# Softmax reciprocals on GpSimd as a power of −1, and neighbourhood scores negated and minimised

## The chip, the core and the metric

The kernel runs on one core of one Trainium2 chip. The metric is device time in microseconds (us) of one execution, and the figure compared is the median of repeated runs. Before the change the median of three runs is 1474.62 us, the lowest 1473.72, the highest 1475.12.

The engines have short names in what follows: PE is TensorE (matrix products), PEld its weight loads, DVE VectorE, ACT ScalarE, POOL GpSimd, and SP is SyncE, which issues most DMAs here. Each engine takes its instructions in one fixed order and waits on semaphores for the results of others.

## What is computed

One inference step of a two-layer transformer trunk for two groups of tokens with the same weights: 128 context tokens (the "prompt") and 512 latent tokens on a grid 64 wide. Layer 0 has two sets of attention heads side by side: 8 heads of MLA (keys and values come from a compressed latent) and 8 heads of two-dimensional neighbourhood attention. Layer 1 has 8 heads of grouped-query attention (GQA). A SwiGLU feed-forward block follows each. Latent tokens also read 128 cached context tokens. All attentions end in a softmax over keys:

```python
def attend_blocked(q, k, v, scale):                       # MLA and GQA, blocks of 128 queries
    s = jnp.einsum('bqkgd,bskd->bkgqs', qi, k).astype(jnp.float32) * scale
    p = jax.nn.softmax(s, axis=-1).astype(v.dtype)
    return jnp.einsum('bkgqs,bskd->bqkgd', p, v)

def neighbourhood_attention(q, k, v, k_ctx, v_ctx, rpb):  # one grid row
    s_band = jnp.einsum('bqhd,bikhd->bhqik', q_r, k_band).astype(jnp.float32) * NA_SCALE
    s_band = s_band + bias.transpose(0, 2, 1, 3)[None].astype(jnp.float32)
    s_band = jnp.where(col_mask[:, None, :], s_band, NEG_INF)
    s_ctx = jnp.einsum('bqhd,bchd->bhqc', q_r, k_ctx).astype(jnp.float32) * NA_SCALE
    p = jax.nn.softmax(jnp.concatenate([s_band, s_ctx], axis=-1), axis=-1).astype(v.dtype)
```

Inputs and outputs are 32-bit floats.

## The kernel before

**Arithmetic and layout.** TensorE multiplies in the type `fp32r`. To keep precision each operand is split into a high part (a copy by ACT) and a low part (the operand less its high part, mostly by DVE), and the helper `mm3` (its products are all recorded at L64) adds three products. `unit` does this for weights: a load issued by SP at L165 into one of three buffers, the copy at L173, the subtraction at L174. The argument `lo="g"` puts the subtraction on POOL; only the key weights of MLA, `wm0` to `wm3`, use it. Activations stand feature-major, 640 tokens (512 latents and 128 context) in two halves of 320.

**The softmax of one head.** A head has four tiles of 128 queries (GQA a fifth of 128 x 128; in the other two, one pair of such prompt tiles for two heads, `prompt_pair`). For each tile:

1. PE makes scores in PSUM (`ns`, `ms`, `gs`).
2. DVE finds the maximum of each row and its negative. In MLA (L990) and for the prompt that is one reduction with a negated result (`mn`); in GQA the negated maximum is also multiplied by a factor (L1864, `gb`). In neighbourhood attention one instruction adds mask and bias to the scores, stores the sums in `np` and keeps their maximum (L784, `nm`), and a second negates it (L787, `nn`).
3. ACT computes the exponential with that negative maximum as a bias and accumulates the sum of the row (`nl`, `ml`, `gl`): L788, L992, L1865. The trace shows the reading of that sum as an instruction of its own, ACTIVATION_READ_ACCUMULATOR.
4. `softmax_tail` (L390 to L393): DVE takes the reciprocal of the sum (L392, `nr`, `mr`, `gr`), and POOL multiplies the tile by it (L393, in place).

One head later PE transposes the weights (L68, helper `tr`) into `nt`, `mt` or `gt`, `pt_split` splits these into a high part on ACT (L401, `nts..h`, `mts..h`) and a low part on DVE (L402, `nts..l`, `mts..l`), and PE multiplies with the values (`no`, `mo`, `go`).

**The order.** For each head, pieces of this work are written down in a fixed string: `NA_ORDER`, `MLA_ORDER` and `GQA_ORDER`. `s0` to `s4` are score tiles with their softmax, `t0` to `t4` transposes with their splits, `v0` to `v4` products with the values, and `q`, `k`, `m`, `w`, `u` are projections and weight units of the next head or stage, put between so that PE has work while the softmax passes through the other engines. A scheduler then places each engine's instructions from that order and its own idea of when each is ready, so an instruction that is removed or moved to another engine also shifts others.

**What else POOL does there.** In neighbourhood attention it adds mask and bias tables (L765, `bm`) and scales or copies queries and keys (L719, L744, L746); at the end of it come the splits of `wm0` and on; in MLA it makes the low parts of the queries (L891, `mql`).

Of the kernel before, what the change touches and what calls it, by code (L numbers as in the profile page):

```python
# [11 lines left out]
F32 = mybir.dt.float32  # L12
F32R = mybir.dt.float32r
AF = mybir.ActivationFunctionType
ALU = mybir.AluOpType
# [3 lines left out]
P = 128  # L19
# [11 lines left out]
GQA_SCALE = 128.0 ** -0.5  # L31
EPS = 1e-6
# [19 lines left out]
def body(ctx, tc, xT, vecs, crow, wm0, wm0g1, wm0g, wm1, wA, wNV, wNA, wMK, wMV, wOA, wGQ, wGK, wGV, wOC,  # L52
# [3 lines left out]
    V, S, G = nc.vector, nc.scalar, nc.gpsimd  # L56
# [13 lines left out]
    main = ctx.enter_context(tc.tile_pool(name="main", bufs=1))  # L70
# [5 lines left out]
    tiny = ctx.enter_context(tc.tile_pool(name="tiny", bufs=6))  # L76
# [12 lines left out]
    def bank(name, kind="m"):  # L89
        if kind == "m":  # L90
            return psp.tile([P, 512], F32, tag="m", bufs=4, name=name)
        return ypool["pool"].tile([P, 512], F32, tag=kind, bufs=ypool["tags"][kind], name=name)
# [41 lines left out]
    make_identity(nc, ident)  # L134
    ones = main.tile([P, P], F32, name="ones")
    V.memset(ones, 1.0)
    eps = main.tile([P, 1], F32, name="eps")
    V.memset(eps, EPS)
    lnsc = main.tile([P, 1], F32, name="lnsc")
    V.memset(lnsc, math.log(GQA_SCALE))  # L140

    sel = main.tile([P, 4], F32, name="sel")
    V.memset(sel, 0.0)
# [245 lines left out]

    def softmax_tail(pt, l, name, n):  # L390
        r = tiny.tile([P, 1], F32, tag="r", name=name + "r")
        V.reciprocal(r, l)  # L392
        G.tensor_scalar(pt[:, :n], pt[:, :n], r, 0.0, ALU.mult, ALU.add)  # L393

    def pt_split(ps, n, pool, name, shape=None):
# [29 lines left out]
    def prompt_pair(vs, o, pool, name, sbank):  # L425
# [6 lines left out]
        def first(r, product):  # L432
            def run(spare=None):
                pss = sbank(f"{name}s{r}")[:, :P] if spare is None else spare[:, 0]
                product(pss)
                m = tiny.tile([P, 1], F32, tag="m2", name=f"{name}m{r}")
                V.tensor_reduce(m, pss, AX.X, ALU.max, negate=True)
                l = tiny.tile([P, 1], F32, tag="l2", name=f"{name}l{r}")
                sl = pt[:, r * P:(r + 1) * P]
                S.activation(sl, pss, AF.Exp, bias=m, accum_out=l)  # L440
                softmax_tail(sl, l, f"{name}r{r}", P)
            return run
# [312 lines left out]
    def na_bias(h):  # L755
        gt = ab.tile([P, 32, 15], F32, tag="gt", bufs=1, name=f"gt{h}")
        row = rpbp[h]
        src = bass.AP(tensor=row.tensor, offset=row.offset + 8, ap=[[15, 16], [1, 8], [1, 480]])
        nc.sync.dma_start(gt.rearrange("p a b -> p (a b)"), src)
        bm = bms[h % 2]  # L760
        for v, n0, k0, o in ((0, 0, 0, 0), (0, 128, 16, 128), (1, 0, 0, 0), (1, 128, 16, 256), (2, 0, 16, 256), (2, 128, 0, 128)):
            n1 = n0 + 128
            g0 = gt[:, 31 - k0, 14:15]
            rev = bass.AP(tensor=g0.tensor, offset=g0.offset, ap=[list(g0.ap)[0], [-15, (n1 - n0) // 8], [-1, 8]])
            G.tensor_tensor(bm[:, v, o:o + P].rearrange("p (a b) -> p a b", b=8), rev,  # L765
                            msk[:, v, n0:n1].rearrange("p (a b) -> p a b", b=8), ALU.add)
        return bm

    def na_scores(h, bm, pts):
        p, r = divmod(h, 2)  # L770
        qh, ql, ks = [t[r] for t in nqk[p]]
        mm = tiny.tile([P, 4], F32, tag="mm", bufs=4, name=f"nm{h}")
        ll = tiny.tile([P, 4], F32, tag="ll", bufs=4, name=f"nl{h}")

        def piece(jj):
            banks = [bank(f"ns{h}_{jj}{i}", "y") for i in range(2)]
            for j in (2 * jj, 2 * jj + 1):
                pss = banks[j % 2]
                k0, cq = P * PLACE[j][0], slice(P * j, P * j + P)
                PE.matmul(pss[:, 0:384], qh[:, cq], ks[:, k0:k0 + 384], start=True, stop=False)  # L780
                PE.matmul(pss[:, 0:384], ql[:, cq], ks[:, k0:k0 + 384], start=False, stop=True)
            for j in (2 * jj, 2 * jj + 1):
                pt = ab.tile([P, 384], F32, tag="np", bufs=8, name=f"np{h}_{j}")
                V.tensor_tensor_reduce(pt, banks[j % 2][:, :384], bm[:, (0, 1, 1, 2)[j], :], 1.0, -3.0e38, ALU.add, ALU.max,  # L784
                                       mm[:, j:j + 1])
                nm = tiny.tile([P, 1], F32, tag="nm", name=f"nn{h}_{j}")
                V.tensor_scalar_mul(nm, mm[:, j:j + 1], -1.0)  # L787
                S.activation(pt, pt, AF.Exp, bias=nm, accum_out=ll[:, j:j + 1])  # L788
                softmax_tail(pt, ll[:, j:j + 1], f"nr{h}_{j}", 384)
                pts.append(pt)  # L790
        return [lambda jj=jj: piece(jj) for jj in range(2)]
# [108 lines left out]
    bm = na_bias(0)  # L900
# [5 lines left out]
    for h in range(8):  # L906
        p, r = divmod(h, 2)
# [6 lines left out]
        if h < 7:  # L914
            bm = na_bias(h + 1)
# [62 lines left out]
    def mla_scores(h, pts, beside):  # L978
        r = h % 2
        ll = tiny.tile([P, 4], F32, tag="ll", bufs=4, name=f"ml{h}")  # L980

        def piece(j):
            qh, ql = mqs[h]
            pss = bank2(f"ms{h}_{j}")
            kh, kl = [t[0] for t in k_tiles(r, h // 2)]
            scores(pss, (qh[:, P * j:P * j + P], ql[:, P * j:P * j + P]), kh, kl)
            if j in beside:
                beside[j](pss[:, :, HT:HT + P])
            nm = tiny.tile([P, 1], F32, tag="nm", name=f"mn{h}_{j}")
            V.tensor_reduce(nm, pss[:, :, :HT], AX.XY, ALU.max, negate=True)  # L990
            pt = cp.tile([P, T], F32, tag="mp", bufs=8, name=f"mp{h}_{j}")
            exps[h, j] = S.activation(halves(pt), pss[:, :, :HT], AF.Exp, bias=nm, accum_out=ll[:, j:j + 1])  # L992
            softmax_tail(pt, ll[:, j:j + 1], f"mr{h}_{j}", T)
            pts.append(pt)
        return [lambda j=j: piece(j) for j in range(4)]
# [36 lines left out]
    for h in range(8):  # L1032
        p, r = divmod(h, 2)
# [886 lines left out]
    _, before = mod_side([(1, wm1[G2:], G2)], None)  # L1920
# [172 lines left out]
```

## Time and profile before

| what | value |
|---|---|
| median of three runs | 1474.62 us (1473.72 to 1475.12) |
| span of the profiled execution, first to last instruction | 1475.7 us |
| instructions in it | 25826 |
| chain that ended last: PE / DVE / DMA / ACT / POOL | 75% / 11% / 5% / 5% / 1% |

The page prints for each engine the time in which it was busy, its share of the span and its number of instructions. A second part cuts the span into 40 equal slices, with the busy tenths of each engine:

```profile
PE   5999999999999999999999999999999999999997
DVE  5877788877998889965997878888899898989976
POOL 0046635420000000000000122220000000000000
PEclk9999999999999999999999999999999999999999
```

Each slice is 36.9 us. POOL works in slices 3 to 9, which hold neighbourhood attention and MLA, and in slices 23 to 27, which hold GQA; elsewhere nearly nothing. PE is busy throughout, and its clock is granted in full. Rows of groups read as line, engine, operation, output and inputs with their shapes, count, then busy time in us and the mean of one in ns, then the idle time of that engine just before these instructions and what ended it. Rows of single instructions begin with the start in us and the duration in us. Numbers in names are heads and tiles; the page and the groups by line leave buffer numbers out.

### The profile page before, as it was taken

What the parts mean: (1) busy time and instruction counts of PE and PEld (TensorE: products, weight loads), DVE (VectorE), ACT (ScalarE), POOL (GpSimd) and SP (SyncE); (2) the same over time, 40 slices, a digit from 0 to 9 for tenths busy, and PEclk for the clock granted to TensorE, in tenths of its full rate; (3) what the DMA queues carried; (4) which work ended last, traced back from release to release, by engine and by line L of the source; (5) the groups of instructions that cost most, each with busy time, mean ns of one, the idle gap of its engine ahead of it and who ended that gap; (6) DMA issues with size and microseconds to landing.
All of it is one profiled execution on the core that took longest, in us unless ns stands there. A gap on an engine that the chain in (4) does not pass through costs nothing.

```text
span 1475.7 us, 25826 instructions
## 1 busy us (share of the span) xinstructions
PE 1440.4 (98%) x9764; PEld 1390.5 (94%) x9764; DVE 1235.6 (84%) x2391; ACT 783.4 (53%) x1539; POOL 176.0 (12%) x270
## 2 busy tenths in 40 slices
PE   5999999999999999999999999999999999999997
PEld 3989978889999999999999999989999999999997
DVE  5877788877998889965997878888899898989976
ACT  5446677853755545531223656672656555555443
POOL 0046635420000000000000122220000000000000
PEclk9999999999999999999999999999999999999999
DMA  9643431025164555568764300115245555548572
GB/s 374 217 153 125 144 115 44 15 90 182 48 214 164 169 167 173 183 232 315 240 224 143 100 30 30 43 39 190 86 167 181 182 175 184 176 145 297 181 267 72
DMA packets 79637, 231.49 MB, mean 157 GB/s; under 512 B 8856, under 2 KB 13240, under 8 KB 79128
## 3 DMA queue, kind: packets, MB, share of 16 engines
q1 hardware_dynamic: 77152, 225.43, 44.8%
q10 hardware_dynamic: 1944, 3.48, 0.7%
q8 instruction: 76, 1.25, 0.3%
q0 software_dynamic: 416, 0.93, 0.2%
q14 instruction: 49, 0.40, 0.1%
HBM read 193.15 MB, written 36.66 MB: 156 GB/s over the span
## 4 chain that ended last, share of the span: by engine, by line
PE 75%; DVE 11%; DMA 5%; ACT 5%; issue 3%; POOL 1%; DVEq 0%; ACTq 0%; SPq 0%; POOLq 0%
PE fg L64 14%; PE fd L64 6%; PE fgo L64 5%; PE fo L64 5%; PE gq L64 4%; PE fu L64 3%; PE fdo L64 2%; PE gs L64 2%; PE go L64 2%; PE nq L64 2%; PE nk L64 1%; PE fuo L64 1%; DVE junk L1660 1%; PE gt L68 1%; DMA wm<-in_wm 1%
## 5 line engine op out<-in xcount | busy, mean ns | idle before, releaser
L1660 DVE SCALAR_TENSOR_TENSOR junk<-wm,cb 128x1024 bf16<-128x1024 f32 x88 | 107.3, 1220 | 6.7 <-DMA wm<-in_wm 5.5
L64 PE MATMUL gq<-h10h,wgq 128*128 128x320 f32 x256 | 66.3, 318 | 0.0
L267 POOL TENSOR_SCALAR h10h<-h10t,gs,mods 128x320 fp32r<-128x320 f32 x4 | 4.0, 992 | 430.8 <-DVE h10t L261 428.5
L1400 ACT ACTIVATE wY<-s 128x1024 fp32r<-128x1024 f32 x38 | 40.3, 1061 | 25.7 <-PE fg L64 21.1
L1928 POOL TENSOR_TENSOR xr<-xw,fn1rs 128x320 f32<-128x320 f32 x2 | 1.7, 858 | 412.9 <-ACT fn1rs L235 412.9
L1400 ACT ACTIVATE wZ<-s 128x1024 fp32r<-128x1024 f32 x38 | 40.1, 1055 | 15.4 <-PE fd L64 10.3
L1401 DVE TENSOR_TENSOR wZ<-s,wZ 128x1024 fp32r<-128x1024 f32 x38 | 46.3, 1220 | 1.4
L1401 DVE TENSOR_TENSOR wY<-s,wY 128x1024 fp32r<-128x1024 f32 x38 | 46.3, 1219 | 0.3
L64 PEld LDWEIGHTS gq<-h10h,wgq 128*128 128x128 f32 x256 | 45.3, 190 | 0.6
L1509 DVE TENSOR_TENSOR sg<-up,sg 128x640 f32<-128x640 f32 x38 | 31.3, 823 | 15.8 <-ACT sg L1508 14.8
L1508 ACT ACTIVATE sg<-fg 128x320 f32<-128x320 f32 x38 | 16.7, 439 | 48.4 <-PE fg L64 48.4
L64 PE MATMUL gq<-h10l,wgq 128*128 128x320 f32 x128 | 39.8, 311 | 0.0
L1530 ACT ACTIVATE p<-fd 128x320 f32<-128x320 f32 x38 | 16.6, 438 | 42.5 <-PE fd L64 42.5
L1865 ACT ACTIVATE gp<-gs,gb,rq 128x640 f32<-128x640 f32 (+1 forms) x40 | 31.8, 796 | 13.4 <-DVE gb L1864 12.0
L64 PE MATMUL fg<-h01E,wW 128*128 128x320 f32 x228 | 36.6, 309 | 1.1 <-DVE g L1540 1.1
L64 PE MATMUL fg<-h01N,wZ 128*128 128x320 f32 x228 | 36.6, 309 | 0.3 <-ACT p L1528 0.3
L64 PE MATMUL fg<-h01C,wY 128*128 128x320 f32 x228 | 36.6, 309 | 0.2 <-ACT u L1534 0.2
L64 PE MATMUL fg<-h11N,wZ 128*128 128x320 f32 x228 | 36.7, 309 | 0.0
L64 PE MATMUL fg<-h01q,wX 128*128 128x320 f32 x228 | 36.7, 309 | 0.0
L64 PE MATMUL fu<-h11q,wX 128*128 128x320 f32 x228 | 36.6, 309 | 0.0
L64 PE MATMUL fd<-h11q,wZ 128*128 128x320 f32 x228 | 36.6, 309 | 0.0
L64 PE MATMUL fd<-h01q,wZ 128*128 128x320 f32 x228 | 36.5, 309 | 0.0
(3421 smaller groups left out, 5313.5 us busy)
## 6 DMA issues: line engine op xcount, KB each, us to landing
wm<-in_wm SPq DMA_DIRECT2D x48, 512.0 KB, 4.3
mraw<-in_wm SPq DMA_DIRECT2D x8, 1024.0 KB, 13.2
mraw<-in_wm SPq DMA_DIRECT2D x14, 512.0 KB, 3.7
wmv<-in_wm0g SPq DMA_DIRECT2D x8, 512.0 KB, 4.0
wm<-in_wm0g SPq DMA_DIRECT2D x8, 512.0 KB, 5.4
ruo<-in_wFO SPq DMA_DIRECT2D x8, 512.0 KB, 4.1
rgo<-in_wFO SPq DMA_DIRECT2D x8, 512.0 KB, 5.5
x<-in_xT SPq DMA_DIRECT2D x8, 320.0 KB, 5.2
```

What stands on the lines that cost most here:

```text
L64: cls.last = nc.tensor.matmul(*a, **k)
L68: cls.last = nc.tensor.transpose(*a, **k)
L267: G.tensor_scalar(h[:, c0:c1], t, self.gsl[:, k, 0:1], self.ml[:, self.sh + k, 0:1], ALU.mult, ALU.add)
L1400: S.activation(h, src, AF.Copy)
L1401: V.tensor_tensor(w_, src, f(h), ALU.subtract)
L1508: last = S.activation(sg[:, 0:HT], g[:, :HT], AF.Silu, scale=-1.0)
L1509: V.tensor_tensor(sg, up, sg, ALU.mult)
L1530: S.activation(p5, b5[:, :HT], AF.Copy)
L1660: V.scalar_tensor_tensor(junk, raw, 1.0, cb[:, c, :], ALU.mult, ALU.mult, accum_out=mods[l][:, j0 + i, c:c + 1])
L1865: gexp[h, j] = S.activation(dst, src, AF.Exp, bias=nb, scale=rq[:, j:j + 1], accum_out=ll[:, j:j + 1])
L1928: G.tensor_tensor(x[k][:, c0:c1], root[1][k], nrm.rs[:, c0:c1], ALU.mult)
```

## The change

Two edits. In `softmax_tail` the reciprocal is no longer taken by DVE: POOL raises the sum to the power −1, with a column of constants −1 as the exponent, in the instruction ahead of its scaling. In neighbourhood attention the instruction at L784 multiplies the scores by −1 before it adds mask and bias (`bm`) and keeps the minimum, where it kept the maximum of scores times 1 plus `bm`; so it stores negated sums, its minimum is the negative of the maximum, and the exponential takes the stored tile with scale −1 and the minimum as its bias. The separate negation goes. Two small constant tiles and the new −1 share one tile. In the diff of the kernel's text:

```diff
-    eps = main.tile([P, 1], F32, name="eps")
-    V.memset(eps, EPS)
-    lnsc = main.tile([P, 1], F32, name="lnsc")
-    V.memset(lnsc, math.log(GQA_SCALE))
+    consts = main.tile([P, 3], F32, name="consts")
+    eps, lnsc, neg = [consts[:, i:i + 1] for i in range(3)]
+    for t, value in ((eps, EPS), (lnsc, math.log(GQA_SCALE)), (neg, -1.0)):
+        V.memset(t, value)
...
     def softmax_tail(pt, l, name, n):
         r = tiny.tile([P, 1], F32, tag="r", name=name + "r")
-        V.reciprocal(r, l)
+        G.tensor_tensor(r, l, neg, ALU.pow)
         G.tensor_scalar(pt[:, :n], pt[:, :n], r, 0.0, ALU.mult, ALU.add)
...
-                V.tensor_tensor_reduce(pt, banks[j % 2][:, :384], bm[:, (0, 1, 1, 2)[j], :], 1.0, -3.0e38, ALU.add, ALU.max,
+                V.tensor_tensor_reduce(pt, banks[j % 2][:, :384], bm[:, (0, 1, 1, 2)[j], :], -1.0, 3.0e38, ALU.add, ALU.min,
                                        mm[:, j:j + 1])
-                nm = tiny.tile([P, 1], F32, tag="nm", name=f"nn{h}_{j}")
-                V.tensor_scalar_mul(nm, mm[:, j:j + 1], -1.0)
-                S.activation(pt, pt, AF.Exp, bias=nm, accum_out=ll[:, j:j + 1])
+                S.activation(pt, pt, AF.Exp, bias=mm[:, j:j + 1], scale=-1.0, accum_out=ll[:, j:j + 1])
                 softmax_tail(pt, ll[:, j:j + 1], f"nr{h}_{j}", 384)
```

The edits shorten the text, so lines past L787 stand two lower afterwards (L788 becomes L786, L990 becomes L988). Three places show how the engines' rows change. The first is POOL at the end of neighbourhood attention, where the scalings of the last head (`np_0` to `np_3`, and `npp3p` for the prompt) stand between the splits of the MLA weights `wm0` and `wm1`. Before:

```order
L393 TENSOR_SCALAR np_0_2384<-np_0_2384,nr_0r 128x384
L174 TENSOR_TENSOR wm_2555<-wm0r,wm_2555 128x768
L393 TENSOR_SCALAR np_1_2392<-np_1_2392,nr_1r 128x384
L393 TENSOR_SCALAR np_2_2431<-np_2_2431,nr_2r 128x384
L393 TENSOR_SCALAR np_3_2439<-np_3_2439,nr_3r 128x384
L393 TENSOR_SCALAR npp3p<-npp3p,npp3r0r 128x128
L174 TENSOR_TENSOR wm_2984<-wm1r,wm_2984 128x768
```

The same place after the change, where the rows at L392 are the powers:

```order
L392 TENSOR_TENSOR nr_0r<-nl_2321,consts 128x1
L393 TENSOR_SCALAR np_0_2336<-np_0_2336,nr_0r 128x384
L392 TENSOR_TENSOR nr_1r<-nl_2321,consts 128x1
L393 TENSOR_SCALAR np_1_2342<-np_1_2342,nr_1r 128x384
L174 TENSOR_TENSOR wm_2499<-wm0r,wm_2499 128x768
L392 TENSOR_TENSOR nr_2r<-nl_2321,consts 128x1
L393 TENSOR_SCALAR np_2_2379<-np_2_2379,nr_2r 128x384
L392 TENSOR_TENSOR nr_3r<-nl_2321,consts 128x1
L393 TENSOR_SCALAR np_3_2385<-np_3_2385,nr_3r 128x384
L392 TENSOR_TENSOR npp3r0r<-npp3l_2421,consts 128x1
L393 TENSOR_SCALAR npp3p<-npp3p,npp3r0r 128x128
L174 TENSOR_TENSOR wm_2920<-wm1r,wm_2920 128x768
```

A power stands ahead of each scaling, and the split of `wm0` stands behind two scalings where it stood behind one.

The second place is ACT at the same point. L401 makes the high parts of transposed weights, L846 copies a cached key, L788 is the exponential, L173 the high part of a weight. Before:

```order
L401 ACTIVATE nts_0h<-nt_0_2400 128x512
L401 ACTIVATE nts_1h<-nt_1_2409 128x512
L401 ACTIVATE npp2pth<-npp2t 128x256
L846 ACTIVATE ckph<-ckvr_753 128x128
L788 ACTIVATE np_0_2384,nl_2369<-np_0_2384,nn_0_2386 128x384
L173 ACTIVATE wm_2555<-wm0r 128x768
L788 ACTIVATE np_1_2392,nl_2369<-np_1_2392,nn_1_2394 128x384
L401 ACTIVATE nts_2h<-nt_2_2463 128x512
```

ACT there after the change:

```order
L401 ACTIVATE nts_0h<-nt_0_2348 128x512
L401 ACTIVATE nts_1h<-nt_1_2357 128x512
L786 ACTIVATE np_0_2336,nl_2321<-np_0_2336,nm_2320 128x384
L786 ACTIVATE np_1_2342,nl_2321<-np_1_2342,nm_2320 128x384
L401 ACTIVATE npp2pth<-npp2t 128x256
L844 ACTIVATE ckph<-ckvr_753 128x128
L173 ACTIVATE wm_2499<-wm0r 128x768
L401 ACTIVATE nts_2h<-nt_2_2407 128x512
```

Both exponentials move ahead of two smaller copies and of the copy of `wm0r`, and read the minimum `nm` itself.

The third place is DVE between the first and the second head of MLA. L990 is the row maximum, L889 a step of the queries, L476 and L867 are low parts. Before:

```order
L990 TENSOR_REDUCE mn_3_2953<-ms_3_2946 128x1
L392 RECIPROCAL mr_2r<-ml_2869 128x1
L990 TENSOR_REDUCE mn_0_2974<-ms_0_2967 128x1
L392 RECIPROCAL mr_3r<-ml_2869 128x1
L889 TENSOR_TENSOR mqt_2993<-mq_2981,tq 128x320
L476 TENSOR_TENSOR oNs0l<-oN_1177,oNs0h 128x640
L392 RECIPROCAL mr_0r<-ml_2964 128x1
L990 TENSOR_REDUCE mn_1_3004<-ms_1_2997 128x1
L392 RECIPROCAL mr_1r<-ml_2964 128x1
L867 TENSOR_TENSOR kTl_2542<-mk_3011,kTh_2540 64x512
```

DVE there after the change:

```order
L988 TENSOR_REDUCE mn_3_2889<-ms_3_2882 128x1
L988 TENSOR_REDUCE mn_0_2910<-ms_0_2903 128x1
L887 TENSOR_TENSOR mqt_2929<-mq_2917,tq 128x320
L476 TENSOR_TENSOR oNs0l<-oN_1177,oNs0h 128x640
L988 TENSOR_REDUCE mn_1_2940<-ms_1_2933 128x1
L865 TENSOR_TENSOR kTl_2486<-mk_2947,kTh_2484 64x512
```

The four reciprocals are gone and the rest keeps its order. PE's order changes at a few places at the end of MLA only, and that of SP's queue not at all.

## Prediction, made before the changed kernel ran

> **What bounds the kernel now.** First the busy shares on the page, then a table of three stretches of time in which the softmaxes run: neighbourhood attention (112 to 212 us), MLA (222 to 320) and grouped-query attention (850 to 990). Columns: window, length, and busy time of each engine with its count.
>
> ```profile
> PE 1440.4 (98%) x9764; PEld 1390.5 (94%) x9764; DVE 1235.6 (84%) x2391; ACT 783.4 (53%) x1539; POOL 176.0 (12%) x270
> ...
> 112.00:212.00 100.00, 96.98 (x725) 86.98 (x724) 77.80 (x261) 69.28 (x187) 60.09 (x113) 0.98 0.39 129
> 222.00:320.00 98.00, 93.58 (x607) 82.95 (x607) 85.17 (x180) 77.63 (x179) 49.51 (x56) 1.00 0.09 28
> 850.00:990.00 140.00, 138.44 (x931) 130.67 (x930) 115.70 (x254) 93.47 (x216) 32.99 (x40) 0.99 0.10 31
> ```
>
> TensorE (PE) is the engine that fills the program. In the three stretches it is idle for 3.0, 4.4 and 1.6 us, 9.0 together. That is roughly what a lighter VectorE (DVE) can win: the change touches nothing outside them but two constants at the start. GpSimd (POOL) looks free over the program, 12%, but is at 60% in the first stretch and 51% in the second.
>
> Next, what PE waits for inside the stretches. First and second stretch, in this order; columns: who waits, for what, total us, times, longest.
>
> ```profile
> PE no L64 <- DVE nts_0l L402: 1.7, 1, 1.7
> PE mk L64 <- DVE nm L784: 0.9, 1, 0.9
> ...
> PE ms L64 <- ACT mp L992: 1.5, 2, 1.0
> PE mo L64 <- DVE mts_4l L402: 1.4, 3, 1.1
> PE mo L64 <- DVE mts_3l L402: 0.6, 3, 0.2
> PE mo L64 <- DVE mts_0l L402: 0.5, 2, 0.3
> ```
>
> So where PE stands still, DVE (splitting transposed weights into high and low parts) or ScalarE's exponential is late. The chain of waits between 222 and 320 us shows this more sharply:
>
> ```profile
> by line: ACT mp L992 11.3%; issue 10.7%; DVE mn L990 9.2%; PE mo L64 7.6%; PE ms L64 7.2%; PE mt L68 6.2%; PE mq L64 3.5%; PE mk L64 3.2%; PE oa0a L64 3.0%; DVE mts_0l L402 3.0%; DVE mts_4l L402 2.8%; ACT oaw L173 2.4%; ACT mts_2h L401 2.3%
> ...
> 240.44 0.16 DVE mpp0r1r L392
> ...
> 301.45 0.16 DVE mr_2r L392
> ```
>
> The MLA stretch is set by a relay: scores on PE, row maximum on DVE (`mn`), exponential on ACT (`mp`), split on DVE (`mts`). Its chain runs through eight reciprocals (first and last shown, 0.14 to 0.17 us each, 1.3 together). The chains of the other two stretches hold three each.
>
> **The change part by part.** Reciprocals leave DVE: 40 in each stretch, 120 in all.
>
> ```profile
> L392 DVE RECIPROCAL nr_0r<-nl x8: 144/152/164, 115.2 to 203.0; 128x1 f32<-128x1 f32 x8
> ...
> L392 DVE RECIPROCAL gr_2r<-gl x8: 155/164/165, 859.3 to 983.6; 128x1 f32<-128x1 f32 x8
> ...
>   ACT gp L1865: 9.7, 12
>   ACT np L788: 4.1, 12
>   ACT mp L992: 3.8, 8
> ```
>
> At about 0.158 us each that is 120 x 0.158 = 19 us of DVE time. The last three rows are idle time of DVE in front of a reciprocal, while ACT finishes the sum it needs: 9.7, 4.1 and 3.8 us in the third, first and second stretch. DVE takes its work in order, so this idle time goes too, unless the next instruction waits for the same ACT result.
>
> *MLA.* On the chain: -1.3 us. Of the 3.8 us of idle time I count 0.3, since DVE makes up about that share of the chain (from the row by line: 15% in its three large DVE entries, the rest in small ones): -1.2, an estimate whose ends are 0 and -3.8.
>
> *GQA.* Three reciprocals on the chain: -0.5 us. The 9.7 us of stalls lie beside a PE that is 98.9% busy; I count them at nothing, and were that cover gone, PE's 1.6 us of idle time would be the price.
>
> *Neighbourhood attention.* Three more on the chain: -0.5 us. Here 32 negations also go (minimum of negated scores in place of maximum, a constant swapped in an instruction that stays, and a scale of -1 in an exponential that was there):
>
> ```profile
> L787 DVE TENSOR_SCALAR nn<-nm x32: 126/148/155, 114.1 to 205.6; 128x1 f32<-128x1 f32 x32
> ```
>
> That is 4.7 us of DVE, and each exponential starts a DVE step earlier. No negation stands on the chain and PE is 97% busy there: nothing, with PE's 3.0 us of idle time as the far end.
>
> *What POOL gets.* 40 powers in each stretch, each followed by the scaling that was there already and now waits for POOL's own result. No row of this trace shows a power, so bounds from the nearest rows:
>
> ```profile
> L2073 POOL MEMSET const-float32-0.0<- 128x1 f32 x1 | 0.1, 98 | 0.2 <-issue 0.2
> ...
> L765 POOL TENSOR_TENSOR bm<-gt,msk 128x128 f32<-128x128 f32 x48 | 22.7, 499 | 13.2 <-DVE nm L784 9.4 <-DMA gt<-in_rpbp 3.5
> L891 POOL TENSOR_TENSOR mql<-mqt,mqh 128x320 fp32r<-128x320 f32 x16 | 14.0, 873 | 10.3 <-ACT mqh L890 10.3
> ...
> L174 POOL TENSOR_TENSOR wm<-wm2r,wm 128x768 fp32r<-128x768 f32 x1 | 1.8, 1834 | 10.4 <-ACT wm L173 10.4
> ```
>
> The lower end is 0.10 us, one column written. From 320 to 768 columns a two-input operation grows by 961 ns, 2.15 ns a column, which leaves 0.19 us for one column of addition. A power is more work than an addition; the nearest row is the 0.50 us one, and I take **0.4 us**, with 1.83 as the far end. Load of POOL: 60.1 + 16 = 76 of 100 us, 49.5 + 16 = 66 of 98, 33 + 16 = 49 of 140. It fits.
>
> Latency decides too, since the transposes need the scaled weights. The last scaling of a head against the first transpose after it, second head boundary of MLA:
>
> ```profile
> 242.18 0.19 ACT L992 ACTIVATION_READ_ACCUMULATOR mp<-ms,mn 128x1 f32 x1
> 243.30 0.15 DVE L392 RECIPROCAL mr_3r<-ml 128x1 f32<-128x1 f32 x1
> 243.55 0.80 POOL L393 TENSOR_SCALAR mp<-mp,mr_3r 128x640 f32<-128x640 f32 x1 [2.48 <-DVE mr_3r L392]
> 244.89 0.27 PE L68 MATMUL mt<-ident,mp 128*128 128x128 f32 x1
> ...
> 304.79 0.19 ACT L992 ACTIVATION_READ_ACCUMULATOR mp<-ms,mn 128x1 f32 x1
> 305.56 0.80 POOL L393 TENSOR_SCALAR mp<-mp,mr_3r 128x640 f32<-128x640 f32 x1 [1.32 <-DVE mr_3r L392]
> 306.03 0.83 PE L68 MATMUL mt<-ident,mp 128*128 128x128 f32 x5
> ```
>
> At the first of these the reciprocal stood behind other DVE work, and 1.18 us passed from sum to scaling; at the second 0.58. In the new order it is a hand-over (about 0.10), the power, and a hand-over (about 0.09): 0.59. So at 0.4 us the path is no longer than now. Only the last head had a shorter one (0.43): +0.2 us. MLA together: -1.3 - 1.2 + 0.2 = **-2.3 us**.
>
> *What moves.* POOL's split of the weights `wm0` stands behind two scalings now instead of one, and ACT's copy for it behind two exponentials. Behind it hangs a load:
>
> ```profile
> 191.64 0.62 ACT L788 ACTIVATE np<-np,nn 128x384 f32<-128x384 f32 x1
> 192.24 0.85 ACT L173 ACTIVATE wm<-wm0r 128x768 fp32r<-128x768 f32 x1
> ...
> 193.32 1.82 POOL L174 TENSOR_TENSOR wm<-wm0r,wm 128x768 fp32r<-128x768 f32 x1
> 195.17 0.33 SPq L165 DMA_DIRECT2D wm1r<-in_wMK  x1
> 198.60 0.85 ACT L173 ACTIVATE wm<-wm1r 128x768 fp32r<-128x768 f32 x1
> 199.47 0.60 ACT L401 ACTIVATE nts_0h<-nt 128x512 fp32r<-128x512 f32 x1
> ...
> 202.37 0.50 PE L64 MATMUL no<-nts_0l,nv 128*128 128x512 f32 x1 [1.67 <-DVE nts_0l L402]
> ```
>
> POOL's split ends, SyncE's queue issues the load of `wm1r` into the freed buffer, ACT copies it, and only then copies `nts_0h`, for whose low half PE waits 1.67 us. In the new order ACT does two exponentials (0.7 each with the read of the sum) and two small copies before `wm0r`, so that copy ends near 194.2 rather than 193.1; POOL's split then ends near 196.1 rather than 195.1. One microsecond late, on a path with nothing to absorb it: **+1.0 us**, with 0 and +2 as ends. The stretch gives -0.5 + 1.0 = +0.5.
>
> **Sum:** -2.3 - 0.5 + 0.5 = **-2.3 us**. The profiled span of 1475.7 us becomes 1473.4; it lies 1.1 above the median of the timed runs, 1474.62, so the forecast there is **1472.3 us**.
>
> *A rule weighed.* Two rows from the MLA stretch:
>
> ```profile
> 276.49 1.21 DVE L174 TENSOR_TENSOR oaw<-oaw1r,oaw 128x1024 fp32r<-128x1024 f32 x1
> 276.67 1.70 POOL L393 TENSOR_SCALAR mp<-mp,mr_2r 128x640 f32<-128x640 f32 x1 [1.58 <-DVE mr_2r L392]
> ```
>
> The scaling takes 1.70 us beside a DVE operation on two SBUF tiles, and 0.80 in the rows above. The Trainium skill, page "SBUF — State Buffer", section "SBUF: two separate sides", says that GpSimd and a VectorE operation with two SBUF inputs share one port pair, which whoever starts first holds for the whole instruction. The trace agrees: the scaling ends 0.67 us after DVE does. By that rule a power can be held as well; one hold of up to 1.2 us at the end of a head would make the sum -1.1 in place of -2.3.
>
> **The rivals.** *POOL becomes the bound (slower).* In the first stretch it has 39.9 us left for 40 powers, so this decides from 1.0 us a power. At 1.2 us: 108.1 of 100, +8.1; the path from sum to transposes is 0.8 us longer, more than the two last head boundaries can take, +1.8; `wm0` waits for two powers, +2.5; the gains of 3.1 stay: +9.3, 1484 us. At the far end, 1.83 us, POOL needs 133 and 123 us in the first two stretches, +55 us. For it: a power is computed by an engine whose plain additions are three times a reciprocal here. Against: one column only.
>
> *The relay tightens (faster).* If DVE's idle time in MLA goes entirely (3.8 in place of 1.2) and the earlier exponentials win half of PE's 3.0 us in the first stretch and of its 1.6 in the third: -2.3 (the forecast) - 2.6 - 2.3 = -7.2, 1467.4; half of the way beyond the forecast, -4.8, is its middle: 1469.8 us. For it: each exponential of the first stretch stands a negation earlier.
>
> *PE hides it.* PE is over 95% busy in all three, and what one wait loses the next gains: -0.3, 1474.3 us.
>
> That the change does not do what it says is ruled out by the order: the powers stand on POOL, the reciprocals are gone from DVE, no negation is left.
>
> **How the numbers follow.** Forecast 0.40 (1470.7 to 1473.6), the relay tightens 0.24, PE hides it 0.13, POOL the bound 0.23. A change under 0.2%, 2.9 us, is about what a measurement of this kernel cannot tell from none. The forecast's own range crosses it: 0.16 faster, 0.24 same. Faster: 0.16 + 0.24 = 0.40; same: 0.24 + 0.13 = 0.37; slower: 0.23. The range runs from 1467.4 to 1484, leaving out some 0.05 below and 0.1 above.
>
> **What would show it.** POOL rows `nr`, `mr`, `gr` at L392 near 0.4 us; DVE busy time near 24 us lower (19 + 4.7); no DVE idle time put down to sums at L392; the MLA stretch some 2 us shorter; the load of `wm1r` about 1 us later against the first `mk`, and PE's wait at `nts_0l` longer. Wrong, if a power takes 1 us or more, if PE waits for POOL's scalings, or if the stretches stay the same length though DVE is lighter.

## The result and the profile after

The changed kernel takes 1481.0 us, median of five runs (1479.05 to 1483.22). Five runs of the kernel before had their median at 1474.62 us (1473.72 to 1477.61). The ratio is 1.0038, with a 95% interval of 1.0027 to 1.0048: **slower by 0.38%, about 5.6 us** (the two medians lie 6.4 us apart), where 1472.3 us, 2.3 us less, had been forecast.

The profiled execution after the change, its span and busy times, and the three stretches (same columns as before the change):

```profile
span 1477.2 us, 25760 instructions
...
PE 1440.6 (98%) x9764; PEld 1390.1 (94%) x9764; DVE 1224.7 (83%) x2240; ACT 785.5 (53%) x1539; POOL 244.8 (17%) x390
```

```profile
112.00:212.00 100.00, 96.26 (x726) 85.99 (x725) 69.07 (x181) 68.80 (x184) 81.64 (x151) 1.00 0.40 130
222.00:320.00 98.00, 91.60 (x587) 81.12 (x586) 81.60 (x141) 77.39 (x178) 70.93 (x96) 1.00 0.09 28
850.00:990.00 140.00, 138.71 (x946) 131.35 (x945) 115.50 (x219) 93.22 (x217) 56.59 (x80) 1.00 0.10 32
```

DVE became lighter, as meant, but by 10.9 us over the program (8.7 in the first stretch) and not by the forecast's 24. The forecast added up the durations of the instructions that go. Short instructions of DVE overlap with their neighbours in the trace; in the kernel before, for instance (start, duration, instruction):

```profile
122.16 0.27 DVE L713 SCALAR_TENSOR_TENSOR nql<-nq,nqh 64x128 fp32r<-64x128 f32 x1
122.36 0.14 DVE L392 RECIPROCAL nr_0r<-nl 128x1 f32<-128x1 f32 x1
122.42 0.13 DVE L787 TENSOR_SCALAR nn<-nm 128x1 f32<-128x1 f32 x1
122.48 0.67 DVE L402 TENSOR_TENSOR nts_1l<-nt,nts_1h 128x512 fp32r<-128x512 f32 x1
```

The 120 reciprocals last 18.9 us in all, but in only 9.7 us of these is no other row of DVE busy. POOL went from 60 to 82 us of the first 100 and from 50 to 71 of the second 98. PE lost 2 us of work in the second stretch, so it stood still there for longer.

The powers, as rows of the group by line (minimum, median and maximum in ns; first and last start in us), one of each attention:

```profile
L392 POOL TENSOR_TENSOR nr_1r<-nl,consts x8: 542/548/558, 118.8 to 206.9; 128x1 f32<-128x1 f32 x8
...
L392 POOL TENSOR_TENSOR mr_1r<-ml,consts x8: 547/549/961, 230.2 to 312.7; 128x1 f32<-128x1 f32 x8
...
L392 POOL TENSOR_TENSOR gr_1r<-gl,consts x8: 542/547/552, 861.0 to 983.3; 128x1 f32<-128x1 f32 x8
```

A power takes 0.55 us. Who waits for POOL's scalings, in the first two stretches and just past them (who, for what, total us, times, longest):

```profile
PEld nt L68 <- POOL np L393: 3.0, 3, 1.6
PE nt L68 <- POOL np L393: 2.3, 2, 1.4
```

```profile
PEld mt L68 <- POOL mp L393: 3.6, 3, 1.9
PE mt L68 <- POOL mp L393: 2.8, 2, 1.7
```

PE and its weight loads wait together, so the two rows of a pair are not to be added. In the kernel before, the only such row is in MLA:

```profile
PEld mt L68 <- POOL mp L393: 0.2, 1, 0.2
```

The wait is new, and it has few places: PE waits 0.87 us at 123.6 us, 1.43 at 203.0, 1.68 at 238.2 and 1.12 at 318.6. The third of them, on POOL's timeline at the start of MLA (start, duration, instruction):

```profile
230.17 0.55 POOL L392 TENSOR_TENSOR mr_1r<-ml,consts 128x1 f32<-128x1 f32 x1
230.82 0.80 POOL L393 TENSOR_SCALAR mp<-mp,mr_1r 128x640 f32<-128x640 f32 x1
231.59 0.56 POOL L392 TENSOR_TENSOR mpp0r0r<-mpp0l,consts 128x1 f32<-128x1 f32 x1
232.24 0.37 POOL L393 TENSOR_SCALAR mpp0p<-mpp0p,mpp0r0r 128x128 f32<-128x128 f32 x1
232.58 1.85 POOL L174 TENSOR_TENSOR wm<-wm3r,wm 128x768 fp32r<-128x768 f32 x1
234.38 0.55 POOL L392 TENSOR_TENSOR mr_2r<-ml,consts 128x1 f32<-128x1 f32 x1
235.03 0.88 POOL L393 TENSOR_SCALAR mp<-mp,mr_2r 128x640 f32<-128x640 f32 x1
235.89 0.86 POOL L889 TENSOR_TENSOR mql<-mqt,mqh 128x320 fp32r<-128x320 f32 x1
236.72 0.55 POOL L392 TENSOR_TENSOR mr_3r<-ml,consts 128x1 f32<-128x1 f32 x1
237.36 0.80 POOL L393 TENSOR_SCALAR mp<-mp,mr_3r 128x640 f32<-128x640 f32 x1
```

```profile
238.22 0.77 PE L68 MATMUL mt<-ident,mp 128*128 128x128 f32 x5 [1.68 <-POOL mp L393]
```

Apart from 0.10 us between a power and its scaling, POOL is never idle in these rows: its work stands in a queue. The sum that `mr_3r` needs was read off by 232.99 us, and its power starts at 236.72. Ahead of it stood the split of `wm3`, another tile's power and scaling, and `mql`. From the end of a power to the start of its scaling there are 0.10 us, so each tile takes POOL 0.55 + 0.10 = 0.65 us more than it did.

**What a single trace hides.** The span grew by only 1.5 us between the two profiled executions, a quarter of the measured loss. The profiled execution after the change was the fastest of its five (1479.05 us, with a span of 1477.2). If the span before, 1475.7, is likewise 1.85 us short of the timed figure, it stands for about 1477.5 us, near the slowest of the five before. Two traces can't give the total, then, and single stretches need care with the granted clock (third column from the end). Below are the kernel before (two rows), the one after, and the run that only negates the scores, where it is 1.00:

```profile
180.00:212.00 32.00, 29.25 (x214) 25.14 (x214) 28.38 (x88) 27.73 (x72) 16.64 (x26) 0.95 0.35 112
850.00:1000.00 150.00, 148.44 (x994) 139.84 (x993) 120.47 (x261) 97.52 (x223) 32.99 (x40) 0.99 0.13 45
```

```profile
20.00:50.00 30.00, 28.55 (x230) 24.13 (x230) 22.48 (x63) 13.72 (x31) 0.00 (x0) 0.89 0.90 338
```

```profile
850.00:1000.00 150.00, 148.63 (x1004) 139.84 (x1003) 120.76 (x262) 97.66 (x223) 32.94 (x40) 1.00 0.15 50
```

In a dip the clock grants PE 1.5 to 3.5 us less than the length of the window (32 x 0.05 = 1.6 in the first row, 150 x 0.01 = 1.5 in the second, 30 x 0.11 = 3.3 in the third). Which of these three windows have one changes from execution to execution; the rows of nines on the page before are too coarse to show its two dips. Before and after, the dips come to about the same, 3.1 and 3.3 us, so they don't explain the small growth of the span; but they fall into different stretches. GQA looked 1.6 us shorter after the change; all of that was the dip of the trace before.

### The profile page after: what moved, and what is told of

The parts are those of the page before. It is cut to its first block, busy times and chain, and to the rows that moved or that the text cites. A ratio compares the mean times of both kernels' runs of the same rounds, so it can differ in the third digit from the quotient of the medians.

```text
span 1477.2 us, 25760 instructions
## 1 busy us (share of the span) xinstructions
PE 1440.6 (98%) x9764; PEld 1390.1 (94%) x9764; DVE 1224.7 (83%) x2240; ACT 785.5 (53%) x1539; POOL 244.8 (17%) x390
## 4 chain that ended last, share of the span: by engine, by line
PE 82%; DVE 6%; ACT 4%; DMA 4%; POOL 2%; issue 2%; DVEq 0%; ACTq 0%; SPq 0%; POOLq 0%
PE fg L64 19%; PE fd L64 9%; PE fgo L64 5%; PE fo L64 5%; PE fu L64 4%; PE gq L64 3%; PE fdo L64 2%; PE gs L64 2%; PE go L64 2%; PE nk L64 2%; PE fuo L64 1%; PE gt L68 1%; DMA mraw<-in_wm 1%; PE nq L64 1%; PE mod L64 1%
## 5 line engine op out<-in xcount | busy, mean ns | idle before, releaser
L64 PE MATMUL fg<-h11q,wX 128*128 128x320 f32 x228 | 36.5, 309 | 0.0
```

Source lines behind the costliest of these rows:

```text
L64: cls.last = nc.tensor.matmul(*a, **k)
```

## The experiments

Two accounts stood against each other at first. Q: GpSimd's queue is what costs. R: what costs is the order, since without the negation the scheduler puts ACT's exponentials of neighbourhood attention ahead of other work. Each edit below is against the changed kernel.

**The negated scores alone** (`neg_only`):

```diff
-        G.tensor_tensor(r, l, neg, ALU.pow)
+        V.reciprocal(r, l)
```

> The neighbourhood scores are negated and minimised as in the change, the reciprocals stay on VectorE. Theory Q (GpSimd's queue is what costs: a power of 0.55 us and a hand-over of 0.1 ahead of each scaling, on an engine that was 60% busy): no power, no loss; 1472.5 to 1475 us, no wait of PE for a scaling (POOL np or mp, L393) over 0.3 us. Rival R (the order: without the negation the scheduler puts ACT's exponentials ahead of its splits and weight copies in neighbourhood attention, and that is what costs): most of the loss of 5.6 to 6.4 us is here, 1479 to 1482 us.

Measured: 1477.05 us beside 1476.28 for the kernel before on the same chip, ratio 1.0004 (0.9995 to 1.0012). No loss that can be told from none, where R had 1479 us and more: R falls. The time is 2 us above Q's range too, but the kernel before ran slower there as well, and PE's waits for scalings are as short as before (0.2 us of PEld, one place).

**The powers alone** (`pow_only`): the tensor_tensor_reduce, the negation and the exponential of the kernel before are put back.

> All reciprocals go to GpSimd as powers, the maximum is still negated by an instruction of its own. Q: slower than before by about what the full change loses, 1479 to 1483 us, with waits of PE for scalings of 3 us or more together. R: the order is nearly that of before, so 1473 to 1476 us.

Measured: 1483.45 us beside 1476.28, ratio 1.0043 (1.0028 to 1.0059). The loss is the powers'. The negation's removal is worth nothing measurable, with the powers or without.

**The powers by stage** (`pow_na`, `pow_mla`, `pow_gqa`), each with the negated scores:

```diff
-        G.tensor_tensor(r, l, neg, ALU.pow)
+        G.tensor_tensor(r, l, neg, ALU.pow) if name[0] == "n" else V.reciprocal(r, l)
```

> The negated scores, and powers on GpSimd in neighbourhood attention alone; MLA and GQA keep VectorE's reciprocals. Q: the loss of neighbourhood attention and the first scalings of MLA behind its backlog, without the gain of some 1.7 us that the trace shows in GQA: 1478 to 1481 us. R: 1479 to 1482 us, like the negated scores alone.

> The negated scores, and powers on GpSimd in MLA alone. Q (GpSimd's queue): the wait of 1.9 us for the first head's scalings, behind the split of a weight, and 1.1 us more at the last head, less what VectorE wins: ratio to before 1.001 to 1.002, and the three stages alone (NA +3.7 us, this, GQA 0) add up to the full change's 5.6. If MLA gains what was forecast (-2.3 us), 1472 to 1475 us.

> The negated scores, and powers on GpSimd in GQA alone, where GpSimd has work for 33 of 140 us. Q: no loss in the first two stretches, and GQA shorter by 1 to 2 us as in the trace of the full change: 1471.5 to 1474 us. R: the loss by order less GQA's gain, 1477 to 1480 us.

Measured: neighbourhood attention 1479.61 us, ratio 1.0025 (1.0013 to 1.0037); MLA 1477.78 us, 1.0010 (1.0000 to 1.0020); GQA 1476.58 us, 1.0000 (0.9991 to 1.0010). The first two are where Q had them. The gain that R and Q both allowed GQA, 1 to 2 us, isn't there. The waits for scalings in the two that lose, neighbourhood attention first:

```profile
PEld nt L68 <- POOL np L393: 3.4, 3, 2.0
```

```profile
PEld mt L68 <- POOL mp L393: 4.1, 4, 2.1
```

**The price of the operation** (`mult`). The multiplication leaves the softmax undivided:

```diff
-        G.tensor_tensor(r, l, neg, ALU.pow)
+        G.tensor_tensor(r, l, neg, ALU.mult)
```

> The full change with a multiplication of the sum by -1 in place of the power, on the same engine at the same place; the weights are then scaled by the negated sum, so no softmax is divided. If the price is that of the power's function, a row takes 0.1 to 0.25 us instead of 0.55, and by Q the loss falls to less than half: 1475.5 to 1478 us. If it is what any instruction of one column costs on GpSimd, rows stay near 0.5 us and the time at 1480 to 1482 us.

Measured: 1474.97 us beside 1475.72, ratio 0.9993 (0.9984 to 1.0002).

```profile
L392 POOL TENSOR_TENSOR mr_1r<-ml,consts x8: 185/191/193, 226.7 to 308.7; 128x1 f32<-128x1 f32 x8
```

With the order of every engine unchanged, an instruction of 0.19 us in place of 0.55 takes the whole loss away, more than Q had expected. The stretches agree, at full clock in both traces: 109.8 us in neighbourhood attention and 99.6 in MLA, against 111.2 and 101.6 in the full change. PEld waits for scalings of neighbourhood attention for 1.0 us instead of 3.0:

```profile
PEld nt L68 <- POOL np L393: 1.0, 1, 1.0
```

It is the power's duration, 0.36 us above a multiplication's, that counts.

**Other work taken off POOL.** Against Q stood P: the way of each tile itself is longer, whether POOL is crowded or not. First the additions of mask and bias (`bias_dve`):

```diff
-            G.tensor_tensor(bm[:, v, o:o + P].rearrange("p (a b) -> p a b", b=8), rev,
+            V.tensor_tensor(bm[:, v, o:o + P].rearrange("p (a b) -> p a b", b=8), rev,
```

> The full change, with the 48 additions of mask and bias (0.5 us each) on VectorE, so GpSimd has some 24 us less to do in neighbourhood attention. Q: the powers no longer stand behind them, the median wait of a power for GpSimd there falls from 1.9 us to under 0.5, PE's waits at 122 and 124 us go, 1477 to 1479.5 us. Rival P (not the queue but the longer way of each tile itself, power and hand-over, 0.65 us, is what costs): 1480 to 1482.5 us.

Measured: 1477.14 us beside 1475.72, ratio 1.0004 (0.9995 to 1.0012). POOL's busy time in the first stretch fell to 70 us. PE's waits near 122 and 124 us are gone; one, at 199 us behind the split of `wm0`, is left (a power of 1.52 us stands ahead of it too), and the median wait of a power for POOL fell from 1.9 us to 0.9, not to 0.5:

```profile
PEld nt L68 <- POOL np L393: 2.0, 1, 2.0
```

Then the splits of MLA's key weights (`wm_dve`):

```diff
-            wmk[p] = unit(wMK[p], 768, f"wm{p}", lo="g")
+            wmk[p] = unit(wMK[p], 768, f"wm{p}", lo="v")
```

> The full change, with the four low parts of MLA's key weights (1.83 us each on GpSimd) on VectorE. Q: PE's waits for scalings of 1.7 us at 203 us and 1.9 us at 238 us, which stood behind these splits, go or shrink below 0.6: 1477.5 to 1479.5 us. P: nothing changes, 1480 to 1482.5 us.

Measured: 1478.69 us beside 1475.72, ratio 1.0020 (1.0010 to 1.0029). The time is as Q had it, but the two waits of PE only shrank, to 1.2 and 1.1 us: behind the split stood more powers and scalings. Both together (`relief`):

> The full change, with both the mask additions and the weight splits on VectorE. Q (GpSimd's queue): one by one they took 5.0 and 2.7 us off the loss of 5.6 us (ratios 1.0004 and 1.0020 against 1.0038); if the waits they remove are different ones, both together reach 0.998 to 1.000 of before, 1472.5 to 1476 us. If they removed the same waits, 1.0003 or more, 1476 to 1478 us.

Measured: 1474.95 us beside 1475.88, ratio 0.9989 (0.9980 to 0.9998). P would have kept the loss, so P alone can't be the account. But not every wait of PE for a scaling is gone; neighbourhood attention first:

```profile
PE nt L68 <- POOL np L393: 0.7, 1, 0.7
PE mt L68 <- POOL mp L393: 2.2, 2, 1.1
```

The control (`neg_bias_dve`) has VectorE's reciprocals and the additions on VectorE:

> The control: negated scores, reciprocals on VectorE, and the mask additions on VectorE too. Q: there are no powers to stand behind them, so it is like the negated scores alone, ratio 0.9995 to 1.001. If moving the additions is a gain of its own, whatever the reciprocals do, 0.996 to 0.998, and the run that moved them says nothing of a queue.

Measured: 1474.56 us beside 1475.88, ratio 0.9989 (0.9980 to 0.9997), between the two ranges. So the additions moved are worth 0.15% where there are no powers (1.0004 to 0.9989) and 0.34% where there are (1.0038 to 1.0004); only the difference, some 2.8 us, can be the powers' standing behind them, and the four intervals together leave nearly 3 us to each side of it. With the additions moved, the powers still cost 0.15% (1.0004 against 0.9989). With the splits moved as well, `relief` is level with the control at 0.9989, though MLA is 0.9 us longer in its trace and neighbourhood attention 0.9 us shorter; what the splits on VectorE are worth without powers was not run.

**The middle heads of MLA** (`pow_mid`), where POOL has no backlog:

```diff
-        G.tensor_tensor(r, l, neg, ALU.pow)
+        G.tensor_tensor(r, l, neg, ALU.pow) if name[:3] in ("mr2", "mr3", "mr4", "mr5", "mr6") else V.reciprocal(r, l)
```

> The negated scores, and powers on GpSimd for MLA's third to seventh heads alone, where in the traces a power waits 0.08 us for GpSimd and a tile's way is 1.53 us from sum to scaled weights instead of 1.24. Q: nothing lost, the stretch within 0.4 us of that with VectorE's reciprocals, ratio 0.9995 to 1.0008. P (the longer way of a tile): five eighths of MLA's loss of 1.5 us or so, ratio 1.0010 or more. Were the forecast's relay right, a gain of some 1.4 us: 0.999.

Measured: 1475.9 us beside 1475.88, ratio 0.9996 (0.9987 to 1.0004). The ratio speaks against P (1.0010 or more) and can't tell Q from the forecast's relay; the stretch can. Its length runs from the first start of a score product to the last start of a value product of the last head. The rows give these for the run that only negates, for this run, and for the full change:

```profile
L64 PE MATMUL ms<-kTh,mqh x48: 302/309/418, 220.7 to 299.6; 128*128 128x320 f32 x48
...
L64 PE MATMUL mo<-mts_4l,mv x8: 392/471/503, 244.4 to 321.1; 128*128 128x512 f32 x8
```

```profile
L64 PE MATMUL ms<-kTh,mqh x48: 302/309/414, 219.9 to 297.6; 128*128 128x320 f32 x48
...
L64 PE MATMUL mo<-mts_4l,mv x8: 392/476/503, 243.5 to 318.9; 128*128 128x512 f32 x8
```

```profile
L64 PE MATMUL ms<-kTh,mqh x48: 302/309/416, 224.5 to 304.0; 128*128 128x320 f32 x48
...
L64 PE MATMUL mo<-mts_4l,mv x8: 392/423/494, 249.2 to 326.1; 128*128 128x512 f32 x8
```

That is 100.4, 99.0 and 101.6 us. Powers in five heads win 1.4 us; powers in all eight lose 1.2. Q had allowed 0.4 us either way. In these traces, the forecast's relay was right for the middle heads; over all runs with VectorE's reciprocals in MLA the stretch lies between 99.9 and 100.4 us.

**The best that the runs point to** (`mid_bias`): the edits of `pow_mid` and `bias_dve` together.

> The best the runs point to: negated scores, mask additions on VectorE, powers on GpSimd for MLA's third to seventh heads alone. The additions moved gave 0.9989 with VectorE's reciprocals; the middle heads' powers gave 1.2 us in the MLA stretch of the trace (0.9996 against 1.0004). Q: the two add, ratio 0.9975 to 0.9987, 1471.5 to 1474 us where the kernel before runs at 1475.5. If the stretch's gain is only in that trace, 0.9988 to 0.9995.

Measured: 1474.58 us beside 1476.42, ratio 0.9987 (0.9975 to 0.9999), with an MLA stretch of 98.7 us. It beats both kernels, the one before by 0.13%, just clear of the noise; from the additions moved alone (0.9989) it can't be told.

The lengths of the three stretches in the traces, worked out from such rows (first `ns` to first `ms`; first `ms` to last `mo`; first to last `gs`). A star marks a granted clock below 1.00 inside the stretch:

| run | neighbourhood | MLA | GQA |
|---|---|---|---|
| before | 110.2* | 99.9 | 133.3* |
| neg_only | 109.1 | 100.4 | 131.5 |
| neg_bias_dve | 108.6 | 100.0 | 131.4 |
| pow_only | 113.9* | 101.5 | 133.1* |
| full change | 111.2 | 101.6 | 131.7 |
| pow_na | 113.8 | 100.1 | 131.5 |
| pow_mla | 109.5* | 102.1 | 131.5 |
| pow_gqa | 111.6* | 100.3 | 131.7 |
| bias_dve | 108.9 | 101.6 | 131.7 |
| wm_dve | 112.2 | 100.8 | 131.7 |
| relief | 107.7 | 100.9 | 131.6 |
| mult | 109.8 | 99.6 | 131.5 |
| pow_mid | 108.6 | 99.0 | 132.9* |
| mid_bias | 108.3 | 98.7 | 131.5 |

## Why the prediction was wrong

**The step that failed** is the sentence "It fits" after the sum of POOL's load, and with it the point "from 1.0 us a power" from which POOL would decide. The wait of PE for POOL's scalings was therefore put at nothing; that such waits would show the forecast wrong, it had said itself. Both rest on an average over a stretch: 60 us busy and 40 powers in 100 us. The 76 us that the text worked out became 82, not far off. But the sums of a head's four tiles come in bursts: in neighbourhood attention all four within 1.8 us for the first head (116.5 to 118.3), and mostly two by two, 0.6 us apart, for the later ones. Each tile now takes POOL 0.55 + 0.10 + 0.59 = 1.24 us instead of 0.59. Two take 2.5 us and four 5 us, more behind additions or a weight split. A power waited a median of 1.9 us for POOL in neighbourhood attention, and the way from sum to scaled weights grew from 1.9 to 3.6 us on average (2.4 with the scores negated and the reciprocals on DVE). So POOL decided at 0.55 us a power, with 82 of 100 us busy. The rival had the right engine; it too reckoned with a load above 100%, and so set the threshold too high. That its 1484 us, worked out for 1.2 us a power, lies near the 1481.0 measured is luck, and so is it that the range, which ran up to it, holds the result.

**The power's price**: 0.4 us was taken between 0.10 and 1.83; it is 0.55, and the hand-over from the power to its scaling, 0.10, was counted as latency only, not as time of POOL. The estimate of 0.19 us for one column of a plain two-input operation was right to the hundredth (the multiplication's 0.191).

**MLA, -2.3 us**: +1.2 to +1.6 us in the table (100.0 to 100.4 without powers, 101.6 with all). The gain of the shorter relay exists, 1.3 to 1.4 us for five heads (`pow_mid` against `neg_only`, `mid_bias` against `neg_bias_dve`); taken over eight heads that would be 2.1 to 2.2 us, an estimate near the forecast's 2.3. What was left out is the two ends. The second head boundary, where the old and the new way were compared, is a place where POOL is free; the first is not (the 1.68 us above), and at the last head PE waits 1.12 us for a scaling, for the reason given under the held instructions below.

**GQA, -0.5 us**: +0.2 us (131.6 to 131.7 with powers there, 131.4 to 131.5 without, traces with full clock). That the 9.7 us of stalls were hidden behind PE was right.

**Neighbourhood attention, +0.5 us**: +2.1 us against `neg_only`, and more in `wm_dve` (+3.1) and `pow_na` (+4.7). The late split of `wm0` came, further than reckoned: it starts at 198.00 us, 4.7 later than before, of which 2.1 had been lost ahead of the stretch, so 2.6 in place of 1.0. But PE's wait at `nts_0l` didn't grow; it fell from 1.67 to 0.4 us, since PE had already waited 1.43 us one step earlier, for the scalings behind that split. The negations were worth nothing, as forecast.

**Held instructions**, which the forecast weighed at up to 1.2 us and left out of its sum, come as the rows before the change showed them. In a middle head:

```profile
256.07 1.21 DVE L174 TENSOR_TENSOR oaw<-oaw0r,oaw 128x1024 fp32r<-128x1024 f32 x1
256.28 1.40 POOL L392 TENSOR_TENSOR mr_2r<-ml,consts 128x1 f32<-128x1 f32 x1 [1.18 <-ACT mp L990]
```

The power ends 0.40 us after DVE's operation on two SBUF tiles. This agrees with the Trainium skill, page "SBUF — State Buffer", section "SBUF: two separate sides", that whoever starts first holds the port. The same hold is in the run with the middle heads' powers (1.41 us at 250.59 us), and they win all the same. Of the 120 powers 16 are held like this by 0.1 us or more, 10 us in all, and as many of the 120 multiplications in `mult`, 9 us in all, without a loss. At the last head of MLA, though, two held scalings stand right ahead of a wait of PE:

```profile
315.22 1.42 POOL L393 TENSOR_SCALAR mp<-mp,mr_2r 128x640 f32<-128x640 f32 x1
316.61 0.54 POOL L392 TENSOR_TENSOR mr_3r<-ml,consts 128x1 f32<-128x1 f32 x1
317.04 0.82 DVE L476 TENSOR_TENSOR oMs0l<-oM,oMs0h 128x640 fp32r<-128x640 f32 x1 [0.27 <-ACT oMs0h L475]
317.26 1.27 POOL L393 TENSOR_SCALAR mp<-mp,mr_3r 128x640 f32<-128x640 f32 x1
318.58 0.33 PE L68 MATMUL mt<-ident,mp 128*128 128x128 f32 x1 [1.12 <-POOL mp L393]
```

Unheld they take 0.80 us each, so holding makes up 1.1 us of the way to PE's wait of 1.12 us; in `mult` no scaling of the last head's four tiles is held, and PE doesn't wait there. Ahead of the wait at 203.0 us, holding adds 0.7 us (a power takes 0.74 us, a scaling 1.14); ahead of those at 123.6 and 238.2 us it adds nothing. No run takes the holding alone away, so its share of the loss is an estimate from these rows.

The other way round, powers could hold DVE. Group by group, the operations of DVE that the full change and `neg_only` share last 0.4 us longer in all in the full change in neighbourhood attention, 0.1 us shorter in MLA, and 2.8 us longer in GQA, where nothing was lost. So this is not what the change costs.

**The point of departure**: the forecast took the profiled execution as 1.1 us above the median. A timed figure is 1.85 us above the span of the same execution in the run after the change, so like for like the execution was some 3 us above, about what its two dips of the clock took. The forecast is a difference, and its error doesn't come from there. Two small slips don't either: 0.3 of 3.8 us is 1.1 and not 1.2, and the gains named in the text come to 3.3 and not the 3.1 used for the rival.

**What stays open.** The stages' ratios add up to 1.0035 with the negated scores' 1.0004 counted three times over, 1.0027 with it counted once, against the full change's 1.0038; the intervals, 0.001 to each side, allow that, and nothing finer was measured. In the traces, the three stretches of the full change are together 3.5 us longer than those of `neg_only`, where the ratios differ by 5 us; the rest is not placed. Why neighbourhood attention is 2.6 us longer with powers there alone (113.8) than in the full change (111.2) stays open; its trace has a wait of PE of 1.41 us for `nts_0h` at 141.8 us that the full change lacks. Why moving the additions helps where there are no powers was not tested. A scaling of neighbourhood attention starts 1.4 us after its reciprocal on average in `neg_only` and 0.4 us after it in `neg_bias_dve`, so there was a queue on POOL before any power came.

## What to carry to other kernels

Before work goes to an engine with a low busy share, look at the moments at which it arrives: add the new instruction and its hand-over to the burst, with the longest instruction that can stand ahead of it, and compare with the slack of whoever waits. A short operation moved to a lightly used engine can cost more there than it did on the crowded one: here 0.65 us of a queue in place of a 0.16 us instruction that half overlapped with its neighbours. Read the granted clock beside any stretch before a difference of one or two microseconds between two traces is put down to the edit.

## What was not expected of the hardware

On one column of 128 partitions GpSimd takes 0.55 us for a power and 0.19 us for a multiplication, and VectorE 0.16 us for a reciprocal. Between a power and the scaling that reads it there are 0.10 us in which GpSimd does nothing. A scaling or a power that starts during a VectorE operation on two SBUF tiles ends 0.4 to 0.7 us after it (0.40 and 0.67 above). Short VectorE instructions overlap: 18.9 us of reciprocals are 9.7 us of time in which no other is busy. Leaving out the last 10 us, the clock granted to TensorE dips in seven of the fourteen profiled executions, by 1.5 to 3.5 us worth of work, always between 20 and 50, 180 and 212, or 850 and 1000 us.
